# Sparse attention layer: compression issued in quarters, one PSUM bank for its sums, a fourth weight buffer, and queries placed by DMA

## The chip, the cores and the metric

The kernel runs on one core of one Trainium2 chip. The metric is the device time of one launch in microseconds, as the median of several runs; lower is better. TensorE (PE, with its weight loads PEld), VectorE (DVE), ScalarE (ACT), GpSimd (POOL) and SyncE (SP) each work through their own instruction list in order, and wait on semaphores for each other and for DMAs.

## The reference, cut to what matters

Three layers follow each other on 512 tokens of width 1024: a pooling and mLSTM mixer, a sparse attention layer (NSA) with its feed-forward part, and a sliding window layer with its own. The change lies in NSA alone:

```python
q, kc, vc, ks, vs, kw, vw, gt = jnp.split(h @ w_in, splits, axis=-1)
kc, ks, kw = kv(kc, True), kv(ks, True), kv(kw, True)      # True: with rotary embedding
vc, vs, vw = kv(vc, False), kv(vs, False), kv(vw, False)
def compress(t, pe, w1, w2):
    blk = (t[:, :, cidx] + pe).reshape(b, g, n_cmp, CMP_LEN * hd)   # 31 blocks of 32 tokens
    return jax.nn.gelu(blk @ w1) @ w2
kc = compress(kc, cmp_pe[0], cmp_w1[0], cmp_w2[0])
vc = compress(vc, cmp_pe[1], cmp_w1[1], cmp_w2[1])
```

Attention to the compressed keys, to selected blocks and to a window is then added up with gates (a sigmoid of gt), and projected by w_o. There are 16 query heads, handled as 8 pairs, and 4 key groups.

## The kernel before

Activations lie transposed, 128 channels by 512 tokens. A **linear product** (`linear`, L117) multiplies one 128-column tile of weights, eight chunks deep. Each chunk takes three matmuls (`mm3`, L111): high weights by high input, high by low, low by high, since every operand is split into two rounded halves. The weights of one tile are one 512 KB load (`raw`, L91, on SP's queue, three buffers `wr`); `unit` (L96) makes their halves: ACT copies the high half `wh` (L102), DVE subtracts the low half `wl` (L103), three buffers each. So the halves of a product can be made only when the product three before it is done. The first two matmuls of a chunk read `wh`, only the third reads `wl`.

Sums go to eight PSUM banks of one tile each: `mm` (2), `tp` (2), `S` (3) and `po` (1). `wide_ps` (L86) rotates over six of them.

NSA (`nsa`, L636) begins with the split inputs (`mid_norm_x`), two products of the compressed keys, and then the norm (`mid_norm_r`): the column sums of the squares on PE (L152), a chain of small DVE steps, and the broadcast row `rb` (L159, L162). What leaves a product is multiplied by `rb`. In program order there follow:

- `cproj(0)` and `cproj(1)`: the compressed keys (two products made ahead) and values (two more); for keys the rotary step (`rope`, L547, with a half rotation by four small DMAs, L544), then `cmp_blocks` (L915), which builds the 31 overlapping blocks: 24 DVE additions and 8 POOL additions, all on line L928;
- `kproj(0)`: two products, rotary step, `dup_k` (L560: ACT and DVE, high and low halves for two groups);
- `compress` (L931) of keys, then of values: four raw weight loads each, no halves, 64 matmul records each (L940) into two banks, then ACT copies (L945), a gelu of five DVE steps and one ACT Tanh (L949), and the second product (L955 for keys, L962 for values);
- `settle` (the residual rescaled, L764, eight DVE steps), `gate_proj` (an Exp, L756), `vproj(0)`, `qproj(0)`, `cprobs(0)`, `qproj(1)`, `cvals(0)`;
- `att`: 32 steps, one for each pair and 128 queries, with later products as fillers listed in `fill`.

`qproj` places a pair with `stack_q` (L570) twice: for each parity, ACT copies 64 partitions (L575) and DVE subtracts into the other 64 (L576). `stack_pair` (L579), which the sliding window layer uses, does both parities with one ACT copy and one DVE subtraction of 128 partitions, and moves three halves of 64 partitions by DMA on SP (L586).

The framework orders each engine's list when it builds the program. It keeps all data dependences, and takes, as far as the trace shows, the earliest instruction in program order among those that it thinks are ready. The list is then fixed: an engine that meets an instruction whose input is late waits, even where a later one could run.

Of the kernel before, what the change touches and what calls it, by code (L numbers as in the profile page):

```python
# [32 lines left out]
class Model:  # L33
    def __init__(self, ctx, tc, a, out, stop=None):
# [4 lines left out]
        self.wpool = False  # L39
        con = self.con = ctx.enter_context(tc.tile_pool(name="con", bufs=1))  # L40
# [594 lines left out]
    def nsa(self):  # L635
        tc, nc, a = self.tc, self.nc, self.a  # L636
        V, G, S, PE = nc.vector, nc.gpsimd, nc.scalar, nc.tensor
        with tc.tile_pool(name="nsa", bufs=1) as ap:
# [19 lines left out]
            X = {}  # L658
            pre = [self.linear(a["nsa_w"], i, xh, xl, wide=True) for i in range(2)]
# [10 lines left out]
            def kproj(hf, wide=False):  # L670
                for b in range(2):
# [10 lines left out]
            def vproj(hf, wide=False):  # L682
                for b in range(2):
# [3 lines left out]
                    VV[b, hf] = self.v_nat(ap, vT, f"vn{b}", 1)  # L687

            def qproj(p, wide=False):
# [4 lines left out]
                q = [self.stack_q(ap, qf, par, 6) for par in range(2)]  # L694
# [41 lines left out]
            def cproj(kv, pre=None):  # L736
                blk = [ap.tile([128, 8, 124], F32, name=self.n("blk"), tag="p", bufs=4) for _ in range(2)]
                for m in range(2):
                    ps = pre[m] if pre else self.linear(a["nsa_w"], 2 * kv + m, xh, xl, wide=True)
# [8 lines left out]
            def gate_proj():  # L748
# [3 lines left out]
                V.tensor_scalar(gt, gt, self.v("nsa_gate_b")[:48], None, op0=OP.add)  # L752
                gp = self.tp_ps([128, NT, 48])
# [4 lines left out]
                V.reciprocal(gn, gn)  # L758

# [36 lines left out]
            add(4, 0, vproj, 1)  # L796
# [576 lines left out]
```

## Time and profile before

| what | value |
|---|---|
| median of 3 runs | 1666.68 us (1666.2 to 1668.69) |
| profiled execution, time | 1669.42 us |
| profiled execution, span of instructions | 1667.7 us |
| PE busy | 1611.2 us (97%), 7988 matmul records |
| PEld busy | 1309.0 us (78%) |
| DVE busy | 1085.1 us (65%) |
| ACT busy | 796.5 us (48%) |
| POOL busy | 251.7 us (15%) |
| DMA | 145.41 MB, mean 87 GB/s |

Times in the rows are microseconds from the span's start. Matmuls are pipelined, so two neighbouring rows overlap: what a matmul costs is the distance between two starts, not its length. NSA's part up to the attention steps runs from about 394 to 494 us, the attention steps to about 730 us.

### The profile page before, as it was taken

How to read it: one execution, taken by the hardware profiler on the slowest of the kernel's cores; microseconds unless marked ns; L12 is line 12 of the kernel's file. 1: busy time of each engine (PE TensorE's matmuls, PEld its weight loads, DVE VectorE, ACT ScalarE, POOL GpSimd, SP SyncE). 2: the span in 40 equal slices, each digit the busy share in tenths (PEclk: the TensorE clock that was granted, in tenths of full speed). 3: DMA queues.
4: the chain of work that ended last, by engine and by line, in shares of the span. 5: the costliest groups of instructions: out<-in, count | busy, mean ns of one | idle time of the engine just before them, and what ended most of it. 6: DMA issues, size and time to landing. Idle time of an engine off the chain costs nothing. (4 is left out here: it accounts for less than half of the span.)

```text
span 1667.7 us, 21687 instructions
## 1 busy us (share of the span) xinstructions
PE 1611.2 (97%) x7988; PEld 1309.0 (78%) x7988; DVE 1085.1 (65%) x1888; ACT 796.5 (48%) x1525; POOL 251.7 (15%) x310
## 2 busy tenths in 40 slices
PE   7999999999799999999999999998999999999996
PEld 5678788878677777778888888887787888888886
DVE  5776557866779999986555345356988555535447
ACT  4532255554248877764333233145876433323323
POOL 3000000132212122122111001023312111100001
PEclk9999999999999999999999999999999999999998
DMA  4223311123341121103332322233321232322323
GB/s 155 96 77 98 101 65 53 51 84 102 101 131 43 37 62 39 49 24 120 100 101 90 101 90 100 83 107 92 109 77 56 96 101 91 99 98 92 101 89 127
DMA packets 47113, 145.41 MB, mean 87 GB/s; under 512 B 6752, under 2 KB 9056, under 8 KB 47008
## 3 DMA queue, kind: packets, MB, share of 16 engines
q1 hardware_dynamic: 45424, 141.65, 26.6%
q10 hardware_dynamic: 1584, 2.39, 0.5%
q8 instruction: 63, 1.03, 0.2%
q14 instruction: 42, 0.34, 0.1%
HBM read 133.13 MB, written 2.10 MB: 81 GB/s over the span
## 5 line engine op out<-in xcount | busy, mean ns | idle before, releaser
L102 ACT CAST wh<-wr 128x1024 fp32r<-128x1024 f32 (+2 forms) x241 | 247.2, 1026 | 494.5 <-PE S L109 208.0
L103 DVE TENSOR_TENSOR wl<-wr,wh 128x1024 fp32r<-128x1024 f32 (+2 forms) x232 | 282.5, 1219 | 40.4 <-ACT wh L102 39.6
L108 PE MATMUL mm<-xh,wh 128*128 128x512 f32 (+1 forms) x584 | 233.8, 400 | 0.4 <-ACT xh L130 0.4
L109 PE MATMUL mm<-xl,wh 128*128 128x512 f32 (+1 forms) x584 | 232.2, 398 | 2.0 <-DVE xl L134 2.0
L110 PE MATMUL mm<-xh,wl 128*128 128x512 f32 (+1 forms) x584 | 231.8, 397 | 0.0
L108 PE MATMUL S<-xh,wh 128*128 128x512 f32 x512 | 200.4, 391 | 8.3 <-ACT wh L102 8.3
L109 PE MATMUL S<-xl,wh 128*128 128x512 f32 x512 | 200.4, 391 | 0.1
L110 PE MATMUL S<-xh,wl 128*128 128x512 f32 x512 | 200.0, 391 | 0.0
L109 PEld LDWEIGHTS mm<-xl,wh 128*128 128x128 f32 (+1 forms) x584 | 110.3, 189 | 25.6 <-DVE xl L134 3.2
L108 PEld LDWEIGHTS mm<-xh,wh 128*128 128x128 f32 (+1 forms) x584 | 110.4, 189 | 22.6 <-issue 1.0
L110 PEld LDWEIGHTS mm<-xh,wl 128*128 128x128 f32 (+1 forms) x584 | 110.1, 189 | 21.5
L108 PEld LDWEIGHTS S<-xh,wh 128*128 128x128 f32 x512 | 96.6, 189 | 28.4 <-ACT wh L102 8.3
L110 PEld LDWEIGHTS S<-xh,wl 128*128 128x128 f32 x512 | 96.5, 188 | 20.7 <-DVE wl L103 0.8
L109 PEld LDWEIGHTS S<-xl,wh 128*128 128x128 f32 x512 | 96.5, 188 | 20.6 <-DVE xl L134 0.7
L187 POOL TENSOR_TENSOR sq<-sq,sq 128x512 f32<-128x512 f32 x36 | 60.2, 1673 | 159.9 <-ACT sq L182 151.6
L131 DVE TENSOR_TENSOR ptl<-tp,pth 128x512 fp32r<-128x512 f32 (+1 forms) x112 | 73.6, 663 | 6.8 <-ACT pth L130 6.0
L889 ACT ACTIVATE p<-S,nm 128x128 f32<-128x128 f32 (+3 forms) x128 | 67.1, 532 | 10.6 <-DVE nm L885 5.3
L130 ACT CAST pth<-tp 128x512 fp32r<-128x512 f32 (+1 forms) x112 | 62.9, 573 | 18.8 <-PE tp L612 16.0
L1140 POOL MEMSET fa<- 128x2 f32 x44 | 4.2, 98 | 446.8 <-DVE fc L1145 446.8
L108 PE MATMUL S<-gh,wh 128*128 128x512 f32 (+1 forms) x194 | 71.5, 369 | 0.0
L109 PE MATMUL S<-gl,wh 128*128 128x512 f32 (+1 forms) x194 | 71.5, 369 | 0.0
L110 PE MATMUL S<-gh,wl 128*128 128x512 f32 (+1 forms) x194 | 71.5, 369 | 0.0
(435 smaller groups left out, 3545.8 us busy)
## 6 DMA issues: line engine op xcount, KB each, us to landing
wr<-ffn_gu SPq DMA_DIRECT2D x88, 512.0 KB, 3.5
wr<-w_in SPq DMA_DIRECT2D x32, 512.0 KB, 3.3
wr<-ffn_d SPq DMA_DIRECT2D x32, 512.0 KB, 3.4
wr<-nsa_w SPq DMA_DIRECT2D x20, 512.0 KB, 3.5
wr<-ffn_d SPq DMA_DIRECT2D x24, 384.0 KB, 3.0
wr<-w_out SPq DMA_DIRECT2D x16, 512.0 KB, 3.5
rot<-sq SPq DMA_DIRECT2D x92, 64.0 KB, 2.0
wr<-swa_w SPq DMA_DIRECT2D x10, 512.0 KB, 3.4
```

What stands on the lines that cost most here:

```text
L102: nc.scalar.copy(h[:, :cols], r[:, :cols])
L103: (nc.gpsimd if self.wpool else nc.vector).tensor_tensor(l[:, :cols], r[:, :cols], h[:, :cols], op=OP.subtract)
L108: mm(ps, wh, xh, start=first, stop=False)
L109: mm(ps, wh, xl, start=False, stop=False)
L110: mm(ps, wl, xh, start=False, stop=last)
L130: nc.scalar.copy(h, src)
L131: nc.vector.tensor_tensor(l, src, h, op=OP.subtract)
L187: e.tensor_tensor(acc, acc, dst, op=OP.add)
L889: S.activation(t[:, :w], sb[b], AF.Exp, bias=nm[:, 0, h, b:b + 1], accum_out=nm[:, 1, h, b:b + 1])
L1140: G.memset(t[:, 0:2], 0.0)
```

## The change

The compression becomes a generator that stops after each quarter (one weight load, 16 matmul records), after the gelu, and at its end. Both halves of its sums go into one bank, `po`, which the rotation of the wide products leaves out until attention starts (`banks` is 5, then 6). Its gelu tiles get a tag of their own. Three products, no longer two, come ahead of the norm. `gate_proj` and `vproj` become generators too, and the calls are interleaved by hand. `qproj(2)` moves from the second attention step to before attention; the last step of the values' compression and `cvals(0)` move into it. Pairs 2 to 7 are placed by `stack_pair`. The raw weights have four buffers.

```diff
-        self.rot_ps = (self.rot_ps + 1) % 6
+        self.rot_ps = (self.rot_ps + 1) % self.banks
-        r = self.wp.tile([128, 1024], F32, name=self.n("wr"), tag="wr", bufs=3)
+        r = self.wp.tile([128, 1024], F32, name=self.n("wr"), tag="wr", bufs=4)
...
-            pre = [self.linear(a["nsa_w"], i, xh, xl, wide=True) for i in range(2)]
+            self.banks = 5
+            pre = [self.linear(a["nsa_w"], i, xh, xl, wide=True) for i in range(3)]
...
-                q = [self.stack_q(ap, qf, par, 6) for par in range(2)]
+                if p > 1:
+                    q = self.stack_pair(ap, qf, 6, 1)
+                else:
+                    q = [self.stack_q(ap, qf, par, 6) for par in range(2)]
...
-            bk = cproj(0, pre)
+            bk = cproj(0)
             bv = cproj(1)
-            kproj(0, True)
-            self.compress(ap, 0, bk, w2, bd, vbd)
-            self.compress(ap, 1, bv, w2, bd, vbd)
+            kproj(0, 0, True)
+            ck = self.compress(ap, 0, bk, w2, bd, vbd)
+            cv = self.compress(ap, 1, bv, w2, bd, vbd)
+            kproj(0, 1, True)
+            next(ck)
+            gt = gate_proj()
+            next(gt)
+            next(ck)
+            v0, v1 = [vproj(0, b, True) for b in range(2)]
+            next(v0)
+            next(gt)
+            next(ck)
+            next(v1)
+            next(v0)
+            next(ck)
             settle()
-            gate_proj()
-            vproj(0, True)
+            next(v1)
             qproj(0, True)
+            next(cv)
+            next(ck)
+            qproj(1, True)
+            next(cv)
             cprobs(0)
-            qproj(1)
-            cvals(0)
+            qproj(2, True)
+            next(cv)
+            next(cv)
+            self.banks = 6
...
+            add(0, 1, next, cv)
+            add(0, 1, cvals, 0)
             add(0, 1, cprobs, 1)
-            add(0, 2, qproj, 2)
             add(0, 2, cvals, 1)
...
-        hps = [self.wide_ps([128, 124]) for _ in range(2)]
+        hps = self.o_ps([128, 2, 124])
         for q in range(4):
             w = self.raw(a["cmp_w1"], 4 * kv + q)
...
-                    PE.matmul(hps[m], ..., start=(j == 0), stop=(j == 15))
+                    PE.matmul(hps[:, m], ..., start=(j == 0 and m == 0), stop=(j == 15 and m == 1))
+            if q < 3:
+                yield
```

## Rows read from the trace of the kernel before

**Rows 1.** Busy time of each engine in stretches of NSA: PE, PEld, DVE, ACT, POOL, each with its count of instructions, then the granted clock, the DMA share and GB/s.

```profile
420.80:429.10 8.30, 8.30 (x38) 6.86 (x38) 8.17 (x13) 0.59 (x1) 3.27 (x4) 1.00 0.10 25
429.10:440.00 10.90, 9.27 (x73) 8.59 (x71) 10.75 (x15) 0.58 (x1) 5.91 (x6) 1.00 0.55 171
440.00:452.00 12.00, 4.31 (x36) 3.99 (x35) 7.15 (x13) 8.17 (x16) 0.00 (x0) 0.88 0.32 109
452.00:458.00 6.00, 6.00 (x35) 5.92 (x36) 1.13 (x3) 0.23 (x2) 0.00 (x0) 0.66 0.10 14
500.00:560.00 60.00, 57.27 (x353) 44.91 (x352) 56.54 (x124) 49.17 (x129) 14.70 (x17) 1.00 0.12 32
560.00:720.00 160.00, 158.27 (x958) 124.63 (x958) 150.58 (x321) 126.89 (x328) 30.22 (x36) 1.00 0.16 49
```

**Rows 2.** PE in order of time through the compression: start, length, line, operation, and in brackets the idle time before it with what ended it.

```profile
430.81 0.38 PE L940 MATMUL po<-blk,wr 128*128 128x124 f32 x2
...
437.96 0.48 PE L940 MATMUL po<-blk,wr 128*128 128x124 f32 x2 [1.63 <-DMA wr<-cmp_w]
...
440.02 3.83 PE L940 MATMUL S<-blk,wr 128*128 128x124 f32 x32
445.07 0.46 PE L940 MATMUL S<-blk,wr 128*128 128x124 f32 x2 [1.22 <-DMA wr<-cmp_w]
451.99 1.19 PE L955 MATMUL tp<-gx,w 128*128 128x124 f32 x4 [6.46 <-ACT wh L102]
452.97 4.99 PE L940 MATMUL S<-blk,wr 128*128 128x124 f32 x30
457.72 0.47 PE L108 MATMUL mm<-xh,wh 128*48 128x512 f32 x1
```

**Rows 3.** ACT in order of time, the same columns.

```profile
441.92 1.28 ACT L565 ACTIVATE kd<-kf 64x512 fp32r<-64x512 f32 x2 [10.32 <-DVE kf L558]
...
449.04 0.25 ACT L945 COPY gx<-po 128x124 f32<-128x124 f32 x1
```

**Rows 4.** DVE in order of time, the same columns.

```profile
415.76 0.69 DVE L662 TENSOR_TENSOR cos<-cos,rb 128x512 f32<-128x512 f32 x1
...
418.50 2.37 DVE L558 TENSOR_TENSOR cf<-cf,rot 128x512 f32<-128x512 f32 x2 [0.26 <-POOL rot L556]
420.80 8.29 DVE L928 TENSOR_TENSOR blk<-cf,pe 64x248 f32<-64x248 f32 x12
429.11 1.29 DVE L744 TENSOR_TENSOR cf<-S,rb 128x512 f32<-128x512 f32 x2
430.32 9.65 DVE L928 TENSOR_TENSOR blk<-cf,pe 64x248 f32<-64x248 f32 x12
...
441.20 0.68 DVE L558 TENSOR_TENSOR kf<-kf,rot 128x512 f32<-128x512 f32 x1
...
463.03 1.22 DVE L103 TENSOR_TENSOR wl<-wr,wh 128x1024 fp32r<-128x1024 f32 x1
464.17 5.38 DVE L764 SCALAR_TENSOR_TENSOR H<-H,vec,r 128x512 f32<-128x512 f32 x8
```

**Rows 5.** PE in order of time around the norm, and one product of the keys (425.37 is the start of the next).

```profile
406.28 1.84 PE L152 MATMUL tp<-ones,sq 128*128 128x1 f32 x16
...
414.02 1.05 PE L159 MATMUL tp<-ident,nwy 128*128 128x128 f32 x8
...
419.93 0.39 PE L108 MATMUL mm<-xh,wh 128*128 128x512 f32 x1
...
425.37 0.39 PE L108 MATMUL S<-xh,wh 128*128 128x512 f32 x1
```

**Rows 6.** Two other idle times of PE, in the first and in the sliding window layer: the matmul that ended each (columns as in rows 2).

```profile
25.62 1.56 PE L152 MATMUL tp<-ones,sq 128*128 128x1 f32 x8 [3.64 <-DVE sq L187]
...
1149.88 0.58 PE L1020 MATMUL S<-kd,qs 128*128 128x256 f32 x1 [5.04 <-DVE qs L576]
```

**Rows 7.** Busy times of the stretches right behind the two idle times of rows 6 (columns as in rows 1).

```profile
25.00:30.00 5.00, 4.38 (x15) 3.80 (x16) 3.12 (x12) 0.00 (x0) 0.00 (x0) 0.60 0.25 93
...
1150.00:1155.00 5.00, 5.00 (x24) 4.34 (x25) 2.72 (x5) 3.72 (x10) 4.06 (x2) 0.50 0.32 90
```

**Rows 8.** Groups of instructions in the attention steps, 500 to 720 us, DVE and ACT: line, operation, shapes, count, busy time, mean ns, idle time before.

```profile
L131 DVE TENSOR_TENSOR ptl<-tp,pth 128x512 fp32r<-128x512 f32 x73 | 49.1, 681 | 3.0 <-ACT pth L130 2.3
...
L576 DVE TENSOR_TENSOR qs<-qf,qs 64x512 fp32r<-64x512 f32 x14 | 9.9, 708 | 0.4
...
L130 ACT CAST pth<-tp 128x512 fp32r<-128x512 f32 x73 | 42.2, 589 | 11.8 <-PE tp L612 11.2
...
L575 ACT CAST qs<-qf 64x512 fp32r<-64x512 f32 x12 | 7.4, 619 | 0.2
```

**Rows 9.** The DMAs of `stack_pair` in the sliding window layer: issue on SP in ns (min, median, max), and microseconds to landing.

```profile
L586 SPq DMA_DIRECT2D qs<-ql x14: 462/493/598, 1157.1 to 1229.3; - x14
L586 SPq DMA_DIRECT2D qs<-qs x7: 493/497/510, 1156.4 to 1224.8; - x7
...
DMA to landing us min/median/max: 2.2/2.3/4.2
```

**Rows 10.** ACT's Tanh of the first gelu, and its only table load between 340 and 760 us, ahead of the gates' Exp.

```profile
450.71 0.41 ACT L949 ACTIVATE gt<-gt 128x248 f32<-128x248 f32 x1 [1.26 <-DVE gt L948]
...
472.10 1.28 ACT L756 ACT_TABLE_LOAD   x1
```

More of the change, by code (lines that the diff above doesn't have):

```diff
@@ L668, in nsa, with kproj @@
             K, VV, Q, O = {}, {}, {}, {}
-            def kproj(hf, wide=False):
-                for b in range(2):
+            def kproj(hf, b=None, wide=False):
+                for b in range(2) if b is None else (b,):
                     ps = self.linear(a["nsa_w"], 4 + 8 * hf + b, xh, xl, wide=wide)
@@ L680, in kproj, with vproj @@
                         self.dup_k(kh[:, b], kl[:, b], kf, gp)
-            def vproj(hf, wide=False):
-                for b in range(2):
+            def vproj(hf, b, wide=False):
+                if True:
                     ps = self.linear(a["nsa_w"], 6 + 8 * hf + b, xh, xl, wide=wide)
@@ L734, in wo, with cproj @@
                     V.tensor_tensor(self.H[:, m, :], ps, self.H[:, m, :], op=OP.add)
-            def cproj(kv, pre=None):
+            def cproj(kv):
                 blk = [ap.tile([128, 8, 124], F32, name=self.n("blk"), tag="p", bufs=4) for _ in range(2)]
                 for m in range(2):
-                    ps = pre[m] if pre else self.linear(a["nsa_w"], 2 * kv + m, xh, xl, wide=True)
+                    i = 2 * kv + m
+                    ps = pre[i] if i < 3 else self.linear(a["nsa_w"], i, xh, xl, wide=True)
                     f = ap.tile([128, T], F32, name=self.n("cf"), tag="kf", bufs=2)
@@ L752, in gate_proj @@
                 V.tensor_scalar(gt, gt, self.v("nsa_gate_b")[:48], None, op0=OP.add)
+                yield
                 gp = self.tp_ps([128, NT, 48])
@@ L758, in gate_proj @@
                 V.reciprocal(gn, gn)
+                yield
             def settle():
@@ L765, in settle @@
                                            op0=OP.mult, op1=OP.mult)
-            bk = cproj(0, pre)
+            bk = cproj(0)
             bv = cproj(1)
-            kproj(0, True)
-            self.compress(ap, 0, bk, w2, bd, vbd)
-            self.compress(ap, 1, bv, w2, bd, vbd)
+            kproj(0, 0, True)
[13 more added lines that the diff above has]
+            next(ck)
             settle()
-            gate_proj()
-            vproj(0, True)
+            next(v1)
             qproj(0, True)
+            next(cv)
+            next(ck)
+            qproj(1, True)
+            next(cv)
             cprobs(0)
-            qproj(1)
-            cvals(0)
+            qproj(2, True)
+            next(cv)
+            next(cv)
+            self.banks = 6
             L = lambda f, *x: (lambda: f(*x))
@@ L795, in nsa @@
             add(3, 3, cprobs, 5)
-            add(4, 0, vproj, 1)
+            v2, v3 = [vproj(1, b) for b in range(2)]
+            add(4, 0, next, v2)
+            add(4, 0, next, v3)
+            add(4, 0, next, v2)
+            add(4, 0, next, v3)
             add(4, 0, qproj, 6)
@@ L939, in compress @@
                 for m in range(2):
-                    PE.matmul(hps[m], w[:, jj * 256 + m * 128:jj * 256 + m * 128 + 128], blk[j // 8][:, j % 8, :],
-                              start=(j == 0), stop=(j == 15))
-        x = pool.tile([128, 2, 124], F32, name=self.n("gx"), tag="pc", bufs=2)
-        t = pool.tile([128, 2, 124], F32, name=self.n("gt_"), tag="pc", bufs=2)
-        for m in range(2):
-            S.copy(x[:, m], hps[m])
+                    PE.matmul(hps[:, m], w[:, jj * 256 + m * 128:jj * 256 + m * 128 + 128], blk[j // 8][:, j % 8, :],
+                              start=(j == 0 and m == 0), stop=(j == 15 and m == 1))
+            if q < 3:
+                yield
+        x = pool.tile([128, 2, 124], F32, name=self.n("gx"), tag="gx", bufs=2)
+        t = pool.tile([128, 2, 124], F32, name=self.n("gt_"), tag="gx", bufs=2)
+        S.copy(x, hps)
         V.tensor_tensor(t, x, x, op=OP.mult)
@@ L951, in compress @@
         V.tensor_scalar(x, x, 0.5, None, op0=OP.mult)
+        yield
         if kv == 0:
@@ L965, in compress @@
                 V.tensor_copy(vbd[32 * h:32 * h + 31, :, h * 64:h * 64 + 64], ps)
+        yield
     def swa_tables(self):
```

2 lines of the change are left out of this document (1 added, 1 removed).

## The prediction, made before the changed kernel ran

> **What bounds the kernel now.** First the share of busy time: PE is busy nearly everywhere, so only time in which PE waits can be won, and work that only other engines do costs nothing unless PE waits for it. Then the busy times by stretch [rows 1]: the one place where PE falls far off is the compression, 429 to 458 us, where it is idle for 1.6 and then 7.7 us (10.90 - 9.27, 12.00 - 4.31), and the granted clock sinks to 0.66 behind it. Then PE in order of time [rows 2]: three waits, 1.63 and 1.22 us for weight loads and 6.46 us for the gelu of the keys, 9.3 us together. From 430.81 to 457.72 PE does 128 records of L940 and four of L955. At full speed 32 records take 3.83 us, 0.12 each, so 128 take 15.4 and L955 about 1.0; 26.9 - 16.4 gives a loss of **10.5 us**, the slower clock included.
>
> Why the gelu is late is read one engine further back at each step. Its copy runs on ACT at 449.04, behind the highs and lows of kproj, which began at 441.92 after 10.32 us of waiting for DVE [rows 3]. DVE had begun on the norm's row at 415.76 and was never free: two rotary steps, 12 block additions (8.29), two products times the row, 12 more (9.65), kproj's rotary step, ended at 441.9 [rows 4]. So behind the stall stands a **DVE backlog of 26.1 us**, which starts when the norm's row is there (415.76 to 441.88).
>
> Attention, 500 to 720 us, is different: PE is idle for 2.7 + 1.7 = 4.5 of 220 us and DVE for 3.5 + 9.4 [rows 1]. Both are near their limit, PE nearer.
>
> **What the change does, part by part.** The matmuls are the same, but for their order; two ACT copies become one (under 0.3 us, hidden). The gain must come from PE waiting less.
>
> *Three products ahead of the norm.* PE started the column sums at 406.28, when the second product was done, and the broadcast at 414.02 [rows 5]. DVE's row began 9.5 us after the sums (415.76 - 406.28). With the third product earlier in program order, the sums come one product later: 425.37 - 419.93 = 5.44 us. So the whole backlog moves by 5.4: keys' blocks done at 429.1 + 5.4 = 434.5, values' blocks at 440.0 + 5.4 = 445.4, kproj's rotary step at 441.9 + 5.4 = 447.3. PE's own total up to the last product of kproj is unchanged, so it still gets there at 430.8.
>
> *Quarters between products.* PE's list then is: keys' quarter, gate product, quarter, first values product, quarter, second values product, and so on. The low halves decide. Those of the gate product can be made once the product three before is done, about 419; DVE is waiting for the row then (until 421.2), so they slip in ahead of the backlog. Those of the first values product need the first kproj product, done about 425, inside the backlog. DVE took eight steps of L764 in one go [rows 4], and 12 block additions twice, so I let these low halves wait until 447.3, and add 1.22 [rows 4]: 448.5. Until its third matmul, which needs them, PE has two quarters (2 x 16 x 0.12 = 3.8), the gate product (5.4) and two matmuls (0.5): 9.7. So PE idles 448.5 - 430.8 - 9.7 = **8.0 us**, in two pieces: 3.7 ahead of the first quarter (the blocks, 434.5) and 4.3 ahead of the third matmul.
>
> The clock takes its toll. 3.64 us of idle time was followed by a granted clock of 0.60 over 5 us, 5.04 us by 0.50 [rows 6, 7]: about 2.0 and 2.5 us lost. Here two pieces could cost 0 to 4.5. I take 1.0: what PE loses after the first piece it spends in time that it would have idled before the second. Loss 9.0 against 10.5: **-1.5 us**. Behind 448.5 everything comes in time: ACT's copies for kproj took 7.1 us (441.92 to 449.04 [rows 3]), which now ends about 454.5; the gates' transposes come after the first values product (448.5 + 5.0 = 453.5), and the keys' gelu, which held PE for 6.46 us, now has two products behind its last quarter.
>
> *The fourth raw buffer.* Weight loads made PE wait for 2.85 us [rows 2]; this is part of the 9.3. A quarter is now loaded a product ahead. Worth nothing more elsewhere: PE's other waits are for DVE, ACT and POOL.
>
> *Queries by DMA.* For each of six pairs, two DVE subtractions of 0.71 become one of 0.68, and two ACT copies of 0.62 become one of 0.59 [rows 8]: 0.74 and 0.65 us less, 4.4 on DVE and 3.9 on ACT. SP issues 18 more DMAs of 0.5 us, and the third of a pair must wait for the first to land, 2.3 us [rows 9]; weight loads queued behind come up to that much later, which a buffer more (a product of 5.4 us) covers; without that cover it would be 6 x 2.3 = 14 us. A pair is now ready some 5 us later, but is called for at least one attention step before it is used. Since PE leaves only 4.5 us to win, I count a third: **-1.5** (bounds 0 and -4.4).
>
> *The third query product and the values' tail.* `qproj(2)` leaves the attention, where it filled gaps, and fills them earlier. PE's work is the same. The first 60 us of attention had 2.7 us idle, the other 160 only 1.7; with three pairs ready at the start I count **-1.0** (bounds -2.7 and, as a filler is gone, +1.5).
>
> *ACT's tables.* One load of 1.28 us stands ahead of the gates' Exp; the Tanh before it had none, its table being there [rows 10]. Now the Exp comes before both gelus. If Tanh were not in the Exp's table, there would be four more loads, 5.1 us of ACT, about half of it where attention starts. I take 0, since only a Tanh under the older table is seen; 2.6 is the bound.
> The Trainium skill, "ScalarE: Activation LUTs", section "Table sets: the hidden batching unit", lists tanh in the set of exp; by that page no load is added, and without it the sum would be 2.6 us worse. No run here shows that set hold a Tanh yet.
>
> *One bank, one rotation less.* The copy of the sums ends before attention needs `po`. Five banks mean a product reuses a bank 27 us (5 x 5.4) later; the latest reader, kproj's rotary step, is within that. Nothing.
>
> Sum: -1.5 - 1.5 - 1.0 = **-4.0 us**. The profiled execution took 1669.42 us, 1.7 more than its span and 2.7 more than the median, so the sum would make 1665.4 of it; from the median of 1666.7 it gives **1662.7**.
>
> **Rivals.**
> 1. *The quarters fill the gap.* If DVE's low halves for the values product are placed among the block additions, PE waits only for the keys' blocks, 3.7 us and some clock: a loss of about 4.7 in place of 10.5, -5.8, and with the rest -8.3: 1658.4. With no wait at all it is -10.5 - 2.5 = -13, 1653.7. For it: DVE's list is ordered when the program is built, and a gap seen there would be filled. Against it: the block additions depend on nothing of each other, so there is no gap between them.
> 2. *Slower: the gate product's low halves miss their place.* They must be made before DVE turns to the row at 421.2. If they stand behind the backlog instead (447.3 + 0.6), PE has one quarter and two matmuls, 2.4 us, to do until then: idle 14.7, with 2.5 for the clock 17.2, against 10.5: +6.7, with the rest +4.2: 1670.9. It decides once those halves come after 421. For it: the margin is only some 1.5 us, and one product more ahead of the norm pushes everything late. Against it: ACT and DVE have nothing else to do then.
> 3. *The order of lists doesn't change as written.* The framework moves instructions; if it collects the quarters again behind the products, the gelu waits as before, and only attention gains: -1 to -2, 1665.2.
>
> **How the numbers follow.** Forecast 0.47, rival 1 0.27, rival 2 0.14, rival 3 0.12. About 0.2%, 3.3 us, is what a measurement of this kernel can tell from no change. The forecast spreads by some 2.5 us either way (clock, attention), own range 1660 to 1665.5; 0.6 of it, and all of rival 1, is beyond 3.3: 0.28 + 0.27 = 0.55. Slower: most of rival 2 and a little of the table loads: 0.15. The rest is 0.30. The range runs from 1656.5 (rival 1 with some of the clock) to 1669.5, leaving out the best of rival 1 and the worst of rival 2, 0.2 in all.
>
> **What would show it.** Right, if the norm's broadcast comes about 5 us later; if DVE's blocks still stand in two runs of 12, ended near 445; if PE waits for L928 of the keys and then for L103 of DVE in a values product, some 8 us together; if no wait for a weight load of `cmp_w` is left; if NSA's L576 falls to four records. Wrong, if PE has no wait between 425 and 485 (rival 1), if it waits over 12 us (rival 2), if 64 records of L940 follow each other (rival 3), or if new table loads appear.

## The result, and the profile of the changed kernel

The changed kernel took **1679.51 us** (1676.73 to 1683.38) against 1666.44 us of the kernel before on the same occasion: ratio 1.0076, 95% interval [1.006, 1.0092], 12.7 us slower. On a second occasion it was 1.0064 [1.0052, 1.0077], 10.7 us. The forecast was 4.0 us faster, in a range that ends at 1669.5, so sign and range were both missed. The profiled execution took 1676.73 us with a span of 1674.9. It is 2.8 us below its kernel's median, and that of the kernel before was 2.7 above its own, so that the two profiles differ by 7.3 us where the runs differ by 10.7 to 12.7.

First the forecast's own place: the waits of PE in the compression and at the start of attention, changed kernel; line, what it waited for, microseconds in total, times, longest.

```profile
PE po L971 <- issue: 3.5, 1, 3.5
PE S L111 <- DVE wl L104: 2.6, 1, 2.6
PE S L903 <- ACT p L920: 2.4, 2, 2.2
PE tp L988 <- DVE gx L983: 0.9, 1, 0.9
PE S L913 <- ACT p L920: 0.2, 1, 0.2
```

The first two are the two pieces of the forecast, ahead of the first quarter and in the first values product: 3.5 and 2.6 us instead of 3.7 and 4.3. ("issue" means that the profile names nothing that released PE; the keys' blocks ended at 434.15, 0.1 us ahead of the quarter.) The waits for weight loads and the gelu's 6.46 us [rows 2] are gone; 0.9 of the latter is left (L988). What stands behind them, in order of time on PE and then on DVE:

```profile
411.49 1.84 PE L153 MATMUL tp<-ones,sq 128*128 128x1 f32 x16
...
419.23 1.05 PE L160 MATMUL tp<-ident,nwy 128*128 128x128 f32 x8
...
434.26 3.58 PE L971 MATMUL po<-blk,wr 128*128 128x124 f32 x16 [3.52 <-issue]
...
448.20 0.79 PE L111 MATMUL S<-xh,wl 128*128 128x512 f32 x1 [2.55 <-DVE wl L104]
```

```profile
419.29 0.56 DVE L104 TENSOR_TENSOR wl<-wr,wh 128x384 fp32r<-128x384 f32 x1 [0.43 <-ACT wh L103]
420.94 0.69 DVE L663 TENSOR_TENSOR cos<-cos,rb 128x512 f32<-128x512 f32 x1 [1.09 <-ACT rb L163]
...
425.98 8.17 DVE L959 TENSOR_TENSOR blk<-cf,pe 64x248 f32<-64x248 f32 x12
...
435.39 9.69 DVE L959 TENSOR_TENSOR blk<-cf,pe 64x248 f32<-64x248 f32 x12
...
446.92 1.22 DVE L104 TENSOR_TENSOR wl<-wr,wh 128x1024 fp32r<-128x1024 f32 x1
```

The sums and the broadcast are 5.2 us later than in [rows 5], DVE's row 5.2 us later than in [rows 4], and the blocks come in two runs of 12 that end at 434.2 and 445.1. The gate's low halves slip in at 419.29, ahead of the row; those of the values product come at 446.92, behind the backlog. All this is the forecast's picture to within 2 us. So the loss is elsewhere. Busy times by stretch (columns as in [rows 1]); the first three are the stretches between 425 and 510 us in which the granted clock was 0.50, the lower of TensorE's two levels (1.2 GHz instead of 2.4):

```profile
434.10:437.50 3.40, 3.24 (x15) 3.27 (x16) 3.36 (x6) 0.00 (x0) 2.39 (x3) 0.50 0.09 21
447.80:451.20 3.40, 3.00 (x7) 2.42 (x8) 3.30 (x6) 3.28 (x6) 0.00 (x0) 0.50 0.61 164
499.00:502.40 3.40, 3.40 (x10) 2.43 (x11) 3.40 (x13) 3.24 (x12) 0.40 (x1) 0.50 0.86 302
500.00:560.00 60.00, 58.70 (x370) 45.95 (x369) 54.00 (x126) 46.23 (x129) 12.84 (x16) 0.98 0.21 54
560.00:720.00 160.00, 157.61 (x938) 122.86 (x938) 143.83 (x305) 122.01 (x315) 29.60 (x35) 1.00 0.20 56
```

In attention DVE is busy for 9.3 us less than in [rows 1] ((56.54 + 150.58) - (54.00 + 143.83)) and ACT for 7.8 less, while PE's idle time goes only from 4.5 to 3.7 of 220 us. The busy share can't say whether PE comes earlier. For that the two kernels are compared **at equal work**: each matmul shape is given its median distance to the next start in the kernel before, these are summed up along PE's list, and the table says by how many us PE is later (+) or earlier (-) than in the kernel before when the same sum is done. Times are those of the kernel before; all is set to 0 at 425 us, ahead of the first quarter. One profile each, and the two profiles of the changed kernel differ by 0.7 to 1.5, so that differences up to some 1.5 us are noise.

```
                                   485    510    560    640    745    762
changed                           -1.8   +2.5   +1.4   +2.8   +3.4   +6.4
changed, second profile (e5)      -1.1   +3.6   +2.5   +4.2   +4.9   +7.8
rotation set back (e1)            -0.4   +3.8   +2.7   +4.2   +4.8   +5.0
queries by instructions (e2)      -0.7   +3.4   +3.1   +3.2   +3.2   +7.7
two products ahead (e3)           -3.5   -0.3   -1.4   +0.4   +1.0   +4.0
third query product back (e4)     -1.5   +1.1   -0.4   -0.8   -0.1   +4.5
before, rotation shifted (e6)     -0.2   -0.2   -0.2   -0.9   -0.8   +2.1
e1, e2 and e4 together (e7)       -2.9   +1.0   +0.1   +1.9   +1.8   +1.8
e7, two products ahead (e8)       -2.9   -0.5   -1.4   -0.2   -0.2   -0.2
e8, scores a quarter early (e9)   -3.3   -1.5   -2.4   -1.1   -1.2   -1.1
before, queries by DMA (e11)      -0.3   -0.3   -1.1   -1.1   -0.4   -0.2
before, third query early (e12)   -0.3   -0.7   -2.1   -0.4   -0.4   -0.4
e9, four result buffers (e17)     -3.5   -1.4   -2.3   -3.2   -3.7   -3.7
```

Three things stand in the first row. At 485 us the changed kernel is 1.8 us ahead, where the forecast had 1.5. Between 485 and 510, where attention starts, it loses 4.3: PE waits 2.4 + 0.2 us there for ACT's exponents (L903 and L913 above), and 3.40 us at half the clock cost another 1.7. Between 745 and 762, where the feed-forward part starts, which the change doesn't touch, it loses 3.0 in one step. The attention between them costs another 0.9 instead of giving 2.5 back.

Why ACT's exponents are late is read on DVE, in the changed kernel:

```profile
489.70 0.69 DVE L559 TENSOR_TENSOR qf<-qf,rot 128x512 f32<-128x512 f32 x1 [2.03 <-POOL rot L557]
...
493.40 2.36 DVE L104 TENSOR_TENSOR wl<-wr,wh 128x1024 fp32r<-128x1024 f32 x2 [0.20 <-ACT wh L103]
495.68 0.41 DVE L978 TENSOR_TENSOR gt<-gx 128x248 f32<-128x248 f32 x1
496.01 0.42 DVE L907 TENSOR_REDUCE nm<-S 128x2 f32<-128x256 f32 x1
```

The first scores were on PE from 492.46; their maximum (L907), which the exponents need, stands behind the low halves of two weights (L104) and the first step of the values' gelu, and starts 3.5 us later. In the kernel before it starts 0.7 us after the first scores (493.91, and L876 at 494.56).

### The profile page after: what moved, and what is told of

It reads as the page before. It is cut to its first block, busy times and chain, and to the rows that moved or that the text cites. A ratio compares the mean times of both kernels' runs of the same rounds, so it can differ in the third digit from the quotient of the medians.

```text
span 1674.9 us, 21718 instructions
## 1 busy us (share of the span) xinstructions
PE 1616.9 (97%) x7988; PEld 1310.7 (78%) x7988; DVE 1085.8 (65%) x1882; ACT 793.0 (47%) x1517; POOL 248.1 (15%) x310
## 5 line engine op out<-in xcount | busy, mean ns | idle before, releaser
L104 DVE TENSOR_TENSOR wl<-wr,wh 128x1024 fp32r<-128x1024 f32 (+2 forms) x232 | 282.3, 1219 | 43.5 <-ACT wh L103 42.7
L109 PE MATMUL mm<-xh,wh 128*128 128x512 f32 x560 | 224.8, 401 | 0.5 <-ACT xh L131 0.5
L110 PE MATMUL mm<-xl,wh 128*128 128x512 f32 x560 | 222.3, 397 | 0.6 <-DVE xl L135 0.6
L111 PE MATMUL mm<-xh,wl 128*128 128x512 f32 x560 | 222.3, 397 | 0.0
L109 PE MATMUL S<-xh,wh 128*128 128x512 f32 (+1 forms) x544 | 214.2, 394 | 8.1 <-ACT wh L103 7.7
L110 PE MATMUL S<-xl,wh 128*128 128x512 f32 (+1 forms) x544 | 214.4, 394 | 3.7 <-DVE xl L135 3.7
L111 PE MATMUL S<-xh,wl 128*128 128x512 f32 (+1 forms) x544 | 214.0, 393 | 3.0 <-DVE wl L104 3.0
L109 PEld LDWEIGHTS S<-xh,wh 128*128 128x128 f32 (+1 forms) x544 | 102.7, 189 | 30.2 <-ACT wh L103 7.7
L110 PEld LDWEIGHTS mm<-xl,wh 128*128 128x128 f32 x560 | 106.5, 190 | 21.4 <-DVE xl L135 1.0
L111 PEld LDWEIGHTS mm<-xh,wl 128*128 128x128 f32 x560 | 106.2, 190 | 21.0 <-issue 0.4
L109 PEld LDWEIGHTS mm<-xh,wh 128*128 128x128 f32 x560 | 106.4, 190 | 20.5 <-ACT xh L131 1.0
```

Source lines behind the costliest of these rows:

```text
L104: (nc.gpsimd if self.wpool else nc.vector).tensor_tensor(l[:, :cols], r[:, :cols], h[:, :cols], op=OP.subtract)
L109: mm(ps, wh, xh, start=first, stop=False)
L110: mm(ps, wh, xl, start=False, stop=False)
L111: mm(ps, wl, xh, start=False, stop=last)
```

## The experiments

"Change" is (ratio - 1) times 1668 us, with its 95% interval, against the kernel before on the same occasion.

| kernel | median us | ratio | change us |
|---|---|---|---|
| changed, again (e5) | 1678.96 | 1.0064 | +10.7 [8.7, 12.8] |
| e1 rotation set back | 1673.0 | 1.0033 | +5.5 [3.5, 7.5] |
| e2 queries by instructions | 1676.34 | 1.0051 | +8.5 [6.5, 10.5] |
| e3 two products ahead | 1673.92 | 1.0036 | +6.0 [4.0, 8.0] |
| e4 third query product back | 1677.32 | 1.0056 | +9.3 [7.3, 11.3] |
| e6 before, rotation shifted | 1670.97 | 1.0019 | +3.2 [1.8, 4.7] |
| e11 before, queries by DMA | 1669.54 | 1.0011 | +1.8 [0.3, 3.2] |
| e12 before, third query early | 1669.38 | 1.001 | +1.7 [0.2, 3.0] |
| e14 before, four weight buffers | 1666.98 | 0.9995 | -0.8 [-2.3, 0.5] |
| e15 rotation set back later | 1677.71 | 1.0052 | +8.7 [6.2, 11.0] |
| e7 e1, e2 and e4 together | 1669.38 | 1.0008 | +1.3 [0, 2.8] |
| e8 e7 with two products ahead | 1669.37 | 1.001 | +1.7 [0, 3.2] |
| e9 e8, scores a quarter early | 1668.4 | 1.0001 | +0.2 [-1.3, 1.5] |
| e10 e9, low halves on POOL | 1668.43 | 1.0002 | +0.3 [-1.2, 1.7] |
| e13 e9, copies late, 4 buffers | 1666.37 | 0.9988 | -2.0 [-3.5, -0.5] |
| e16 before, 4 result buffers | 1667.96 | 1.0008 | +1.3 [-0.2, 3.0] |
| e17 e9, 4 result buffers | 1665.39 | 0.9988 | -2.0 [-3.5, -0.5] |

### One part of the changed kernel taken back

**e1**, the rotation of the banks:

```diff
+            self.rot_ps = 0
             wo(1, range(8), True)
```

> The changed kernel, with the rotation of the wide PSUM banks set, ahead of the last eight output products of the sparse layer, to the place that it had there in the kernel before. Theory (the number of wide products modulo the banks decides which bank each later product gets, and with it how the last output products end): the 2.9 us that the changed kernel loses between 745 and 765 us of its trace go away, and some of the 1.2 us of the sliding window layer: 2.5 to 4.5 us faster than the changed kernel. Rival (that loss comes from a later end of attention or from the queue of SP): the same time as the changed kernel within 1 us, and its trace still waits for xl at the start of the feed-forward part.

**e2**, all pairs placed by instructions:

```diff
-                if p > 1:
+                if p > 7:
```

> The changed kernel with all query pairs placed by stack_q, as before; nothing else differs. Theory (the DMA placement saves DVE and ACT time that PE does not wait for, and the trace of the changed kernel lost 1.9 us slowly over the attention steps): 0 to 2 us faster than the changed kernel. Rival (it does save, as predicted, and other parts hide it): 1.5 us slower or more.

**e3**, two products ahead of the norm:

```diff
-            pre = [self.linear(a["nsa_w"], i, xh, xl, wide=True) for i in range(3)]
+            pre = [self.linear(a["nsa_w"], i, xh, xl, wide=True) for i in range(2)]
```

> The changed kernel with two products ahead of the norm, not three. Theory of the DVE backlog: the norm's row comes 5.4 us earlier, the wait for the keys' blocks ahead of the first quarter (3.5 us) goes, but the gate product's low halves now stand behind the backlog and PE waits for them until about 442.5: one wait of some 9 us, and the time within 2 us of the changed kernel. Rival (the third product is what cost the time): 4 us faster or more, with no wait over 4 us between 425 and 450.

**e4**, the third query product inside attention again (with the rotation kept as the changed kernel has it there):

```diff
-            qproj(2, True)
...
+            add(0, 2, qproj, 2)
             add(0, 2, cvals, 1)
```

> The changed kernel with the third query product back in the second attention step (the bank rotation is set to what the changed kernel has ahead of its last output products, so that only this differs). Theory (at the start of attention the third product's rotary step, its low halves and the values' gelu stand on DVE ahead of the first maxima, and PE waits 2.2 us and then runs at a lower clock; 3.2 to 4.2 us lost): 2 to 4 us faster. Rival (the values' compression, not the third query product, is what stands in the way): within 1 us of the changed kernel.

**e5**, the changed kernel unchanged:

> The changed kernel as it is, a second time beside kernels that are compared with it. Both theories: 1676 to 1680 us, 9 to 12 us over the kernel before, with a granted clock near 0.988. If it comes out at 1674 or less, the losses that the first profile of it showed are partly that occasion's, and the single edits tried so far took back less than they seemed to.

Against e5's 10.7, e1 takes back 5.2 and e3 4.7; the intervals of both lie clear of e5's. e2 (2.2) and e4 (1.4) do not, and are tried below from the other side. In the table e1's step between 745 and 762 is 0.2 instead of 2.9 to 3.0, and nothing ahead of it moves beyond the noise. e3 has the one long wait of its theory, 7.0 us, but the time of its rival. At 510 us it is 2.8 to 3.9 ahead of the changed kernel, which is most of its 4.7: its lead at 485 is larger, and it has no stretch at the lower clock at the start of attention. The mean granted clock from 490 to 510 us is 0.91 in six of the seven profiles with three products ahead of the norm (both of the changed kernel, e1, e2, e7, e15), and 1.00 in all six with two (e3, e8, e9, e10, e13, e17). e4 is the seventh, with 1.00: its loss at the start of attention is 2.6 instead of 4.3, and the wait for the exponents stays (2.0 us). The 1.7 us that it wins there it loses again at the start of the feed-forward part, where its clock falls and the changed kernel's doesn't:

```profile
756.10:759.50 3.40, 3.40 (x10) 2.62 (x9) 2.93 (x4) 1.04 (x1) 0.00 (x0) 0.50 0.16 18
```

### One part put into the kernel before

**e6**, nothing but the rotation one step on:

```diff
+            self.rot_ps = 1
             wo(1, range(8), True)
```

> The kernel before, with nothing but the rotation of the wide products' banks set one step on ahead of the second output product of the sparse layer, where the changed kernel has it. Theory (the place in the rotation alone makes the loss at the start of the layer behind it): 3 to 4 us slower than before, all of it between 748 and 760 us, TensorE waiting there for VectorE's low halves of x with a bank taken from the score pool. Rival (the loss there comes from what the changed attention leaves late): within 1 us of before, and no step at 748 to 760.

3.2 us slower, and the table has the loss in one step of 2.9, from -0.8 to +2.1, between 745 and 762: the theory holds, for a kernel that differs in nothing but which bank is next. By its span this profile is no longer than that of the kernel before (1667.4 and 1667.7 us), since behind the 5 us wait of the sliding window layer [rows 6] its granted clock was 0.50 for 3.4 us, in the other for 6.8. The runs decide: those with a mean granted clock of 0.990 took 1670.9 us on average, three of e6, and 1668.2, eleven of the kernel before. The waits there, in the kernel with the shift (the kernel before has none in this stretch):

```profile
PE S L109 <- DVE xl L134: 1.7, 2, 1.0
PE S L110 <- DVE wl L103: 0.4, 1, 0.4
```

The banks are others from there on: the last output product lies in `mm` instead of `S`, the first feed-forward product in `S` instead of `mm`. Where that costs is read on DVE, in the low halves of the feed-forward's input (L134, eight of them), the kernel before and then the one with the shift; the additions to the residual (L734) show the banks.

```profile
740.66 0.75 DVE L134 SCALAR_TENSOR_TENSOR xl<-H,vec,xh 128x512 fp32r<-128x512 f32 x1
...
741.93 1.41 DVE L134 SCALAR_TENSOR_TENSOR xl<-H,vec,xh 128x512 fp32r<-128x512 f32 x2
...
743.87 1.84 DVE L134 SCALAR_TENSOR_TENSOR xl<-H,vec,xh 128x512 fp32r<-128x512 f32 x2
...
750.10 0.68 DVE L734 TENSOR_TENSOR H<-S,H 128x512 f32<-128x512 f32 x1
751.24 2.14 DVE L134 SCALAR_TENSOR_TENSOR xl<-H,vec,xh 128x512 fp32r<-128x512 f32 x3 [0.47 <-ACT xh L133]
```

```profile
738.67 0.75 DVE L134 SCALAR_TENSOR_TENSOR xl<-H,vec,xh 128x512 fp32r<-128x512 f32 x1
...
740.53 2.45 DVE L134 SCALAR_TENSOR_TENSOR xl<-H,vec,xh 128x512 fp32r<-128x512 f32 x2
...
743.51 2.44 DVE L134 SCALAR_TENSOR_TENSOR xl<-H,vec,xh 128x512 fp32r<-128x512 f32 x2
...
750.34 0.68 DVE L734 TENSOR_TENSOR H<-mm,H 128x512 f32<-128x512 f32 x1
750.94 4.05 DVE L134 SCALAR_TENSOR_TENSOR xl<-H,vec,xh 128x512 fp32r<-128x512 f32 x3
```

The same eight take 9.7 us instead of 6.1 (0.75 + 1.41 + 1.84 + 2.14 against 0.75 + 2.45 + 2.44 + 4.05): 3.6 more, and PE, which has nothing else to do there, loses 2.9, of which the waits above show 2.1. What makes them longer is seen on POOL, which squares the residual (L187); the stretch of the last three, kernel before and kernel with the shift, and then the first two of the shift's three low halves by themselves:

```profile
752.82 1.71 POOL L187 TENSOR_TENSOR sq<-sq,sq 128x512 f32<-128x512 f32 x1
```

```profile
750.80 1.28 POOL L187 TENSOR_TENSOR sq<-sq,sq 128x512 f32<-128x512 f32 x1
...
752.44 1.34 POOL L187 TENSOR_TENSOR sq<-sq,sq 128x512 f32<-128x512 f32 x1 [0.28 <-ACT sq L182]
```

```profile
750.94 1.69 DVE L134 SCALAR_TENSOR_TENSOR xl<-H,vec,xh 128x512 fp32r<-128x512 f32 x1
752.55 1.77 DVE L134 SCALAR_TENSOR_TENSOR xl<-H,vec,xh 128x512 fp32r<-128x512 f32 x1
```

Each of the two starts 0.1 us behind a square and ends 0.55 us behind that square's end (752.08 and 753.78); the third, with no square beside it, takes 0.74. In the kernel before the three take 0.75, 0.78 and 0.77: the next square starts at 752.82, behind the third, and here it is the square that takes longer (1.71 us, and it ends 1.15 behind the low half). So it matters which of the two engines starts first. Of the eight low halves four start behind a running square with the shift (1.69 to 1.79 us), one in the kernel before (1.18); in the changed kernel there are four (1.70 to 1.79), in e1 one (1.19). The Trainium skill, page "SBUF — State Buffer", section "Who interferes with whom", says that a DVE instruction with two inputs in SBUF contends with a GpSimd instruction that reads SBUF; this trace agrees, 1.69 and 1.77 against 0.74 us. That they came to lie side by side is shown; a kernel without the squares there wasn't run.

**e15**, in the changed kernel the place set back only ahead of the sliding window layer, since e1 gave 5.2 us and the shift alone costs 3.2:

```diff
+            self.rot_ps = (self.rot_ps - 1) % 6
             xh, xl = self.norm_x("norm_mix1")
```

> The changed kernel with the rotation of the banks set back to where the kernel before has it only ahead of the second attention layer, so that the sparse layer's output product and the layer behind it keep the changed place. Theory (the second attention layer loses by its place too, which would explain why the earlier setting back gave 6 us and the shift alone 3): 1675.5 to 1677, 2 to 3 us below the changed kernel. Rival (only the layer behind the sparse one loses, and the other 3 us are an effect of the clock between runs): 1678.5 to 1680, no difference.

2.0 us below e5, with intervals that overlap: not settled. The two numbers that it was to reconcile, 5.2 and 3.2, lie within their intervals of each other too. The profiles show nothing for the theory: from 762 to 1300 us PE falls behind by 1.2 us more in e15, at equal work as in the table, and by 1.2 and 2.5 in the two profiles of the changed kernel.

**e11**, the queries of pairs 2 to 7 by DMA:

```diff
-                q = [self.stack_q(ap, qf, par, 6) for par in range(2)]
+                if p > 1:
+                    q = self.stack_pair(ap, qf, 6, 1)
+                else:
+                    q = [self.stack_q(ap, qf, par, 6) for par in range(2)]
```

> The kernel before with one part of the change alone: the queries of pairs 2 to 7 are placed by DMA. The prediction's step: 1.5 us faster. Theory now (three transfers wait on one another's queue and on ScalarE's and VectorE's halves, and the queries of the next pair come late, a loss that grows through the attention): 1.5 to 3 us slower, a creep between 500 and 740 us and no step. Rival (the creep of the changed kernel comes from the changed order at the start of the attention): within 0.5 us of before.

**e12**, the third query product ahead of attention:

```diff
             cvals(0)
+            qproj(2)
...
-            add(0, 2, qproj, 2)
```

> The kernel before with one part of the change alone: the third query product and its rope stand ahead of the attention, in a bank outside the wide rotation, so that no later bank changes. The prediction's step: 1.0 us faster (bounds 2.7 faster, 1.5 slower). Theory now (that product puts its weight's low half and its rope ahead of the first maxima on VectorE, and TensorE's first banks of scores wait for the exponents behind them): 1.5 to 3 us slower, lost between 485 and 510 us. Rival (the changed kernel's loss there comes from the values' last quarter and its gelu, which this kernel doesn't have there): within 1 us of before or faster.

Both are slower by their time, 1.8 and 1.7 us, with intervals that begin only 0.3 and 0.2 above 0, and neither gains. The places that the theories named are not confirmed: e11's profile shows no creep, and e12's is not behind at 510 (-0.7). So the sign of both steps is shown, if barely; the mechanism isn't. For the start of attention e12's rival is the better one. PE's wait for the exponents there (L903 above, 2.2 us) is 2.0 us in e4 and 1.9 in e7, where the third query product is back inside, and is found neither in the kernel before nor in e12. It comes with the quarters.

**e14**, four weight buffers alone:

```diff
-        r = self.wp.tile([128, 1024], F32, name=self.n("wr"), tag="wr", bufs=3)
+        r = self.wp.tile([128, 1024], F32, name=self.n("wr"), tag="wr", bufs=4)
```

> The kernel before with four instead of three buffers for the raw weights, nothing else. The prediction put this at nothing. Theory: within 1 us of before, since TensorE's long waits end on low halves and results, not on a weight's transfer. Rival (earlier weight transfers stand in SyncE's queue ahead of the partner rows and other small transfers, and these land later): 1 to 2 us slower, spread over all stages.

Nothing that can be measured, as forecast.

### The quarters without the rest, and their gain kept

**e7** takes back what e1, e2 and e4 take back, at once; **e8** is e7 with e3's edit.

> The changed kernel with three parts taken back: the rotation set to where the kernel before has it ahead of the second output product, all queries placed by instructions as before, and the third query product inside the attention again. The quarters, the one bank for the sums and the four buffers stay. Theory (the quarters gain 2 us in their own region and the three other parts made the loss): 1664 to 1667 us, 1 to 3 below the kernel before of the same occasion. Rival (the quarters themselves push VectorE's work to the start of the attention, so the loss there stays, and the clock falls oftener): 1669 to 1673.

> The same as the kernel with the three parts taken back, and two products instead of three ahead of the norm. Two products ahead gave a lead of 3.0 instead of 1.9 us behind the compression region when tried alone. Theory: another 1 us below that kernel, 1663 to 1666. Rival (one long wait in place of two short ones sends the clock down for longer, and the lead is noise of one profile): no difference to it, or up to 2 us slower.

9.4 of the 10.7 us are gone with three parts that the forecast had put at 0, -1.5 and -1.0. Alone, from e6, e11 and e12, they cost 3.2 + 1.8 + 1.7 = 6.7; the 2.7 us between are within the intervals. e8 gives no more than e7, so that e3's 4.7 us belong to the changed kernel as a whole; the lower clock at the start of attention, which e7's profile has and e8's hasn't, doesn't show in the runs of these two. Both kernels are 2.9 us ahead at 485 and have lost 2.4 to 3.9 of it by 510: e7's rival, that the loss stays. DVE at the start of attention in e8, in order of time:

```profile
486.05 0.42 DVE L979 TENSOR_TENSOR gt<-gx 128x248 f32<-128x248 f32 x1
488.22 0.69 DVE L559 TENSOR_TENSOR qf<-qf,rot 128x512 f32<-128x512 f32 x1 [1.75 <-POOL rot L557]
488.83 0.28 DVE L980 TENSOR_SCALAR gt<-gt 128x248 f32<-128x248 f32 x1
489.03 0.42 DVE L908 TENSOR_REDUCE nm<-S 128x2 f32<-128x256 f32 x1
```

The first scores were on PE from 485.32. Their maximum (L908) stands in DVE's list behind the second query's rotary step (L559), which waits 1.75 us for POOL. In the kernel before the same step comes behind the first maximum, and waits 0.38 us:

```profile
494.56 0.41 DVE L876 TENSOR_REDUCE nm<-S 128x2 f32<-128x256 f32 x1
...
497.36 0.69 DVE L558 TENSOR_TENSOR qf<-qf,rot 128x512 f32<-128x512 f32 x1 [0.38 <-POOL rot L556]
```

**e9** is e8 with pair 0's scores of the compressed keys (`cprobs(0)`) one quarter earlier. The second query product stands ahead of the last three quarters in e8 already; now these scores do too:

```diff
             qproj(1, True)
-            next(cv)
             cprobs(0)
             next(cv)
             next(cv)
+            next(cv)
```

> The quarters, one bank and four buffers with two products ahead of the norm, queries and rotation as in the kernel before; and the second query product and pair 0's scores of the compressed keys now stand ahead of the last three quarters of the values' compression. In the same kernel without this move VectorE's first maxima of the attention stood behind that query's rope, whose partner rows had left TensorE only 8 us earlier, and TensorE waited 1.8 us. Theory (the lead of the region is lost at the start of the attention, to this order of VectorE's work): the wait is gone, 1 to 2.5 us less than without the move, 1667 to 1668.5 us, level with the kernel before. Rival (the attention's start is bound by the sum of VectorE's and ScalarE's work there, whatever its order): no difference, 1669 to 1670.

PE's wait falls from 1.8 to 1.3 us, the loss by 510 from 2.4 to 1.8 (table), the time to the kernel before's (+0.2). The direction is the theory's; against e8 the intervals overlap.

**e10** gives two weights' low halves to POOL:

```diff
+            self.wpool = True
             kproj(0, 1, True)
             next(ck)
             gt = gate_proj()
             next(gt)
+            self.wpool = False
```

> The same, and GpSimd instead of VectorE makes the low halves of the weights of the second key product and of the gate product, for which TensorE waits 7.0 us in one piece behind VectorE's blocks. Theory (that wait is VectorE's queue, and GpSimd is idle behind its own blocks): the wait falls to 3 to 5 us, 2 to 4 us less than without the move, 1664 to 1666 us, below the kernel before by 2 to 3. Rival (GpSimd and VectorE slow one another as they did in the rows of before where both ran, and the quarter behind that product waits for the blocks instead): the wait moves to the next quarter and the time stays within 1 us.

PE's waits from 425 to 520, e8 (e9 has the same 7.0) and then e10:

```profile
PE S L111 <- DVE wl L104: 7.0, 1, 7.0
PE S L904 <- ACT p L921: 1.8, 1, 1.8
```

```profile
PE tp L763 <- DVE gt L759: 5.7, 1, 5.7
PE S L111 <- DVE wl L104: 2.2, 1, 2.2
PE S L906 <- ACT p L923: 1.3, 1, 1.3
```

7.0 us became 2.2 + 5.7: the rival. Behind the low halves the next thing that DVE owes PE is the gate's result, just as late.

**e13** goes on in that direction: POOL makes three low halves, the keys' copies and the gate's transposes come behind the values products, and the `kf` tiles (a projection's result while it is worked on) get four buffers instead of two. The copies in `late` are made behind the first values product.

```diff
-                        self.dup_k(kh[:, b], kl[:, b], kf, gp)
+                        late.append((kh[:, b], kl[:, b], kf, gp))
...
-            next(gt)
             next(ck)
             next(v1)
+            next(gt)
...
-  tag="kf", bufs=2
+  tag="kf", bufs=4
```

> The kernel with the second query product early, and four instead of two buffers for the projections' results, GpSimd makes the low halves for the second key product, the gate product and the first values product, the keys' copies into their pairs of halves come behind the first values product instead of ahead of the gate's, and the gate's transposes behind the second values product. In the kernel with only two of these low halves on GpSimd the wait of 7.0 us had become 2.2 for a low half and 5.7 for the gate's result. Theory (both are places in VectorE's and ScalarE's queues, and TensorE has two products that need neither): the waits between 430 and 460 us fall from 7.9 to 3 to 5 us, and the time to 1664 to 1666, 2 to 4 us below the kernel before. Rival (what is gained in this region is given back at the attention's start, where VectorE is the bound, as in the three kernels before this one): the lead shows at 480 us and is gone at 510, 1667.5 to 1669.

2.0 us below the kernel before, but not by the theory: PE's waits in the region are 7.6 us again, on four other things. So the buffers were tried by themselves, **e16** in the kernel before and **e17** in e9.

> The kernel before with four instead of two buffers for the projections' results, nothing else. Theory (the result of a projection waits for a buffer that the queries two products back still hold, in the compression region and in the attention): 1 to 3 us faster than before, 1665 to 1667. Rival (TensorE's waits end on other things, and the gain of the kernel with the copies late came from the moves): within 0.7 us of before.

> The kernel with the second query product early, and the four buffers for the projections' results; the keys' copies and the low halves stay where they were. Theory (the buffers are the gain): 1665.5 to 1667, as the kernel with the copies late. Rival (the moves are the gain): 1668 to 1669, level with the kernel before.

e16 gives nothing, e17 the same 2.0 us as e13, so e13's moves added none. That the buffers were the gain is likely, not shown: the intervals of e17 and e9 overlap. e9 and e17 agree up to 560 us (table); then e17 gains 1.4 where e9 loses 1.2. Attention from 580 to 640 us, e9 and then e17:

```profile
580.00:640.00 60.00, 58.15 (x330) 44.60 (x330) 53.71 (x106) 45.66 (x109) 13.13 (x14) 1.00 0.20 63
```

```profile
580.00:640.00 60.00, 59.54 (x347) 46.55 (x347) 53.54 (x111) 47.67 (x115) 11.90 (x14) 1.00 0.20 56
```

PE is busy 1.4 us more. Of all kernels here only e13 and e17 (median 1665.39 us) are faster than the kernel before by an interval that leaves out 0. Against the kernel before, e17 gains 2.0 us, and against e16, the same buffers without the quarters, 3.3. So the quarters, with all that goes with them in e9, are worth some 2 to 3 us by this estimate, but only without the three other parts and with these buffers.

## Why the prediction was wrong

The signs that the prediction named for being right came about: the broadcast 5.2 us later, two runs of 12 blocks ended at 445.1, the two waits (6.1 us instead of some 8), no wait for a weight load, four records of NSA's `stack_q` subtraction (L577 here). They tested the region of the compression, and the loss lies behind it. By the table it is -1.8 + 4.3 + 0.9 + 3.0 = 6.4 us up to 762.

- **Quarters between products, -1.5: right in its region, wrong behind it.** PE is 1.8 us ahead at 485. PE idled for 6.1 us instead of 8.0, since the first quarter's 16 records took 3.58 us, at a granted clock of 0.50, where full speed makes 1.9 of it [rows 2]: a loss spent in what would have been the second piece, as the prediction had it. What failed is the sentence "Behind 448.5 everything comes in time". It looked at the keys' gelu and the gates, and never asked whose work comes late next: two weights' low halves and a step of the values' gelu now stand ahead of the first maximum in DVE's list (in e4, e7 and e8 it is the second query's rotary step), PE waits 2.6 us at the start of attention, and 1.7 more go to the lower clock behind these waits.
- **One bank, one rotation less, "Nothing": the step that failed most plainly.** It asked only whether a bank is free in time, and counted neither that the rotation is one running index nor that it goes on behind the stretch. The change moves that index by one for all wide products that follow. Price alone 3.2 us (e6), 300 us later, in code that the diff doesn't touch.
- **The third query product, -1.0 (bounds -2.7, +1.5): the sign was wrong**, +1.7 alone (e12), just beyond the bound on that side. The gain was counted from PE's idle time in attention, and a filler's loss only as a bound. Its interval, 0.2 to 3.0, is wide.
- **Queries by DMA, -1.5 (bounds 0 and -4.4): the sign was wrong**, +1.8 alone (e11). Its instructions are as costed, six high and six low halves (below) in place of the 12 and 14 half-sized ones of [rows 8]. In e11 alone, DVE is busy for 4.3 and ACT for 4.9 us less from 500 to 720, so the costs are about right (4.4 and 3.9). The mistake was to turn freed time of an engine that isn't the bound into time, "a third", and to let no loss into the bounds although the pair comes 5 us later.

```profile
L132 DVE TENSOR_TENSOR ql<-qf,qs 128x512 fp32r<-128x512 f32 x6 | 4.1, 683 | 0.2
...
L131 ACT CAST qs<-qf 128x512 fp32r<-128x512 f32 x6 | 3.7, 620 | 2.7 <-DVE qf L559 2.7
```

  (DVE and ACT groups of the changed kernel from 500 to 720 us, columns as in [rows 8].)
- **The fourth raw buffer, nothing: right** (e14), and no weight load of the compression is waited for.
- **ACT's tables, 0: right.** One load, at 456.58, and both Tanh behind it run without another:

```profile
456.58 1.28 ACT L764 ACT_TABLE_LOAD   x1
...
472.84 0.41 ACT L981 ACTIVATE gt<-gt 128x248 f32<-128x248 f32 x1 [2.23 <-DVE gt L980]
...
498.06 0.41 ACT L981 ACTIVATE gt<-gt 128x248 f32<-128x248 f32 x1 [0.43 <-DVE gt L980]
```

  What the prediction took from the Trainium skill, "ScalarE: Activation LUTs", section "Table sets: the hidden batching unit", holds here.
- **The rivals.** None came about: the gap wasn't filled, the gate's low halves kept their place, and the order was as written. The slower rival was looked for where the change is; the losses lay at the next stage's start and one layer on.
- **Open:** where e11 and e12 lose their 1.7 to 1.8 us (in e11's profile PE idles 1.2 us less than before from 500 to 720, and for e12 part may be the clock, on average 0.9887 in its runs against 0.9894), why two products ahead instead of three gives 4.7 us in the changed kernel and nothing in e8, and whether the sliding window layer loses by the rotation too.

## What to carry to other kernels

Where buffers or banks are dealt out by a running index, count how many a change draws, and set the index back where the changed stretch ends: one draw more or less gives every later draw another bank, and here the cost came 300 us later. A stall that is removed gives time only if the next consumer isn't behind the same engine's list, so follow the gain past the stage's end before it is booked. Count freed time on an engine that isn't the bound as nothing until a wait on it is named.

## What the hardware showed beyond expectation

- A DVE low half of 128x512 from two SBUF operands took 0.74 us alone. Where a POOL square of the same size had started first, in five cases of the two kernels of e6, it ended 0.55 us behind the square's end, whenever it had started, and took up to 1.79. Where DVE started first, its 0.77 stayed and the square took 1.71. Four such low halves instead of one go with 2.9 us on PE (e6).
- The time of one program follows the mean granted clock of the run: in four runs the changed kernel had 0.989, 0.989, 0.987 and 0.985 and took 1676.73, 1678.2, 1680.82 and 1683.38 us. A single profile can thus hide a loss of 1 to 3 us that many runs show (e6, e11, e12).
